# Operand addresses modulo 256 in a hybrid decoder trunk: a tile of its own for the first MLP's hidden parts, a pool of its own for the slots

## Chip, cores and metric

One core of one Trainium2 chip runs the whole program. The metric is the device time of one execution in microseconds (us). TensorE multiplies, VectorE (DVE) and ScalarE (ACT) prepare operands and take results out, GpSimd (POOL) and SyncE (SP) mostly issue DMAs. A matmul has two operands in SBUF: the weights, 128 columns that are loaded into the array (PEld in the profile), and the stream, 128 to 512 columns that run through it (PE).

## What is computed

512 tokens of width 1024 run through two layers: a latent attention (MLA) and a gated linear attention (GLA), each followed by a squared-ReLU MLP of width 4096, with RMS norms before each and at the end.

```python
for i in range(DEPTH):                        # DEPTH = 2
    xn = rms_norm(x, norm_mix[i])
    x = x + (mla_mixer(xn, ...) if i % 2 == 0 else gla_mixer(xn, ...))
    xn = rms_norm(x, norm_mlp[i])
    hid = jnp.square(jax.nn.relu(xn @ w_up[i]))
    x = x + hid @ w_down[i]
return rms_norm(x, final_norm)
```

## The kernel before

**Precision.** Operands are float32, and the matmuls run on a rounded form of it (float32r). Every operand is therefore split in a high part (ScalarE rounds it, L110) and a low part (VectorE subtracts, L113), and a product is three matmuls: wh·xh, wh·xl, wl·xh. `piece` splits a weight tile into `wh` and `wl`, each 1024 columns in a room of 1152, at the offset `at`; `signed` (L850, L851) splits with a sign or a gain; `slot("B")` gives one of 16 tiles of 512 columns.

**The MLPs.** Hidden columns come in eight blocks of 512. The first block's up product is plain (`up_first`, L118 to L120, 512 wide). All other up and down products go by a scheme of quadrants with seven products in place of eight (Strassen-Winograd): a block has seven up products (`up_product`, L973) and seven down products (`down_product`, L984 in the first MLP, L991 in the second). In the first MLP a product is 24 matmuls with a stream of 256; in the second MLP a down product is 12 matmuls with a stream of 512. The stream of a first MLP's down product is the hidden data, split by `parts_of_quad` into one of four pairs of slots (`parts_room`); the second MLP uses these pairs as weights. The eighth block's down product is plain again (L1242 in the first MLP, with a spare pair of parts in the buffer of the weight combination S1, tag `comb0`).

`step` treats block 0 with up and down products interleaved; `step_in_halves` treats blocks 1 to 6 with all up products first (168 matmuls in the first MLP), then all down products (168). In the down half the products are, in this order, d11, d22, d12, -d11, -dS1, d12, dS3; each of them needs the high and low parts of a hidden quadrant that VectorE combines shortly before (L1149 to L1163).

**Before block 0.** `quadrants` makes the input's combinations T1 to T4: L895 on ScalarE and L896 to L899 on VectorE for each of four pairs of feature tiles (the buffers are comb 2 to 5), then their split into the tile T (L850, L851). Weight combinations S1, dS1, dS3 and A2 are made by two DMAs each: SP brings one quadrant (L960), POOL adds the other on landing (L951, L962).

**Order.** The code is recorded instruction by instruction; a scheduler then sets each engine's order from the dependences. TensorE, ScalarE, VectorE, POOL and SP each take their own queue in order. A tile's place is fixed when it is allocated: pools are stacked, one behind the other, and a tile's byte address in a partition is the pool's place plus what stands before it, in steps of 32. A `gap` tile takes room and holds nothing.

**Addresses.** For each kind of matmul, the first byte of the stream and that of the weights, modulo 256, as the two programs place them:

| matmuls (line before, after) | number x width | before: stream / weights | after |
|---|---|---|---|
| up products, both MLPs (L973, L993) | 2352 x 256 | 208 / 16 | 208 / 16 |
| down products, first MLP (L984, L1006) | 1176 x 256 | 32 / 16 | 208 / 16 |
| down products, second MLP (L991, L1013) | 588 x 512 | 32 / 32 | 32 / 32 |
| first up products, both MLPs (L118 to L120, L132 to L134) | 192 x 512 | 208 / 208 | 208 / 16 |
| last down product, first MLP (L1242, L1264) | 72 x 512 and 24 x 512 | 32 / 32 and 224 / 32 | 208 / 16 |
| MLA, some of its products (L118 to L120, L680 to L684) | 368 of 128 to 512 | 32/128, 128/32, 192/32, 192/192 | 32 / 32 |
| MLA, GLA, output projections, the rest of L118 to L120 and L421 | about 1200, mostly 512 | 32 / 32 | 32 / 32 |
| GLA, own tiles (L1628, L1650) | 48 and 36 x 256 | 32 / 64 and 128 / 64 | 32 / 32 and 96 / 32 |
| GLA, states (L118 to L120) | 36 x 256 | 32 / 128 | 32 / 96 |

Of the kernel before, what the change touches and what calls it, by code (L numbers as in the profile page):

```python
# [10 lines left out]
F32 = mybir.dt.float32  # L11
# [7 lines left out]
P = 128  # L19
D = 1024  # L20
S = 512
# [29 lines left out]
def trunk_kernel(ctx: ExitStack, tc: tile.TileContext, t_in: dict, out: bass.AP):  # L51
# [39 lines left out]

    def slot(tag, shape=(P, 512)):
        return sb.tile(list(shape), F32R, tag=f"set_{tag}", bufs=16, name=uname("set"))


    X_AT = 44
    both_room = []

    def both_parts(i, at=0):
        if not both_room:  # L100
            both_room.append(sb.tile([P, 16 * S + 128], F32R, tag="set_A", bufs=1, name="set"))
        o = at + i * 2 * S
        return both_room[0][:, o : o + 2 * S].rearrange("p (a t) -> p a t", a=2)
# [39 lines left out]
    W_ROOM, W_AT = 1152, 128  # L143
    AT_X, AT_UP = (X_AT, X_AT), (124, 60)

# [241 lines left out]
    def mla(layer, nrm, first, pools):  # L387
# [3 lines left out]
        X = nrm.out  # L391
        (es, keep), (pre, pp) = pools


# [104 lines left out]
        for t in range(NT):  # L499
            tk = slice(t * P, (t + 1) * P)  # L500
            for hf in range(2):
                p = bank("bc"[hf])
                for k in range(2):
                    mm3(p, cut(CVL[k], slice(None), tk), cut(wv[k], slice(None), 0, slice(hf * 512, hf * 512 + 512)), k == 0, k == 1)
                if (t, hf) == (1, 1):
                    pr = bank("c")
                    for i in range(NT):
                        tr(pr[:, i * 3 * RB : (i + 1) * 3 * RB], rows[:, i * P : (i + 1) * P])
                    cols = keep.tile([P, NT, 3], F32, tag="cols", name="cols")
                    DVE.tensor_copy(cols, pr[:, : NT * 3 * RB].rearrange("p (t a r) -> p t a r", t=NT, a=3)[:, :, :, 0])  # L510
# [125 lines left out]
        HH = MH // 2  # L636
        QR = [f(slot("B", (P, 2, HH, 2, H))) for _ in range(NT)]
        QST = {}
# [176 lines left out]
    def mlp(layer, nrm, nxt=None):  # L815
# [7 lines left out]
        Q = [[[f(slot("B")) for _ in range(2)] for _ in range(2)] for _ in range(2)]  # L823
        parts_room = [(slot("B"), slot("B")) for _ in range(4)]
        turn = [0]
# [60 lines left out]
        def quadrants():  # L886
# [5 lines left out]
            for k in lead:  # L892
# [6 lines left out]
                DVE.scalar_tensor_tensor(t1[:, k], v[:, second], g2, t2[:, k], ALU.mult, ALU.subtract)  # L899
            fast.tile([P, 96], F32, tag="gap", name=uname("gap"))  # L900
            size = KH * 2 * TH
# [73 lines left out]
        def down_product(t, a, parts, start):  # L975
            wh, wl = piece(a, 2, 512, at=AT_UP if nxt else (W_AT, W_AT))
            if nxt:
                for j in range(4):
                    o = t[j // 2][:, j % 2 * TH : (j % 2 + 1) * TH] if isinstance(t, list) else t[:, j * TH : (j + 1) * TH]
                    for k in range(2):  # L980
                        xh, xl = cut(parts, slice(None), slice(k * TH, (k + 1) * TH))
                        a_h, a_l = (w_[:, k, j * P : (j + 1) * P] for w_ in (wh, wl))
                        for n, (w_, x_) in enumerate(((a_h, xh), (a_h, xl), (a_l, xh))):
                            PE.matmul(o, w_, x_, start=start and j % 2 == 0 and k == 0 and n == 0, stop=k == 1 and n == 2, skip_group_check=True)  # L984
                return
# [236 lines left out]
        if nxt:  # L1222
            spare = fast.tile([P, 2 * S], F32R, tag=f"comb{home['S1']}", bufs=1, name=uname("comb"))
            room = [parts_room[(turn[0] + k) % 4] for k in range(3)] + [(spare[:, :S], spare[:, S:])]
# [5 lines left out]
            for c in range(2):  # L1230
# [629 lines left out]
```

## Time and profile before

| | |
|---|---|
| median of 3 runs | 1052.44 us (1051.39 to 1053.14) |
| the profiled execution | 1051.57 us, its span 1049.9 us |
| granted TensorE clock | 0.999 |
| MLA and output projection | 0 to 184 us of the span |
| first MLP | 184 to 506 us (block 0 from 206.7, blocks 1 to 6 from 246.5 to 483.6) |
| GLA and output projection | 506 to 726 us |
| second MLP and final norm | 726 to 1050 us |

How to read it: times are from the start of the span. A row of the time line has the start, the time of the row, engine, line, operation, output<-inputs and the count. Matmuls overlap in the pipeline, so a matmul's own duration (276 ns at 256 columns) is longer than the distance to the next start. A row of windows has the stretch, its length, and for each engine the busy time and, in brackets, the instructions in it. A row of DMA issues ends with the median time from issue to landing.

### The profile page before, as it was taken

What the parts mean: (1) busy time and instruction counts of PE and PEld (TensorE: products, weight loads), DVE (VectorE), ACT (ScalarE), POOL (GpSimd) and SP (SyncE); (2) the same over time, 40 slices, a digit from 0 to 9 for tenths busy, and PEclk for the clock granted to TensorE, in tenths of its full rate; (3) what the DMA queues carried; (4) which work ended last, traced back from release to release, by engine and by line L of the source; (5) the groups of instructions that cost most, each with busy time, mean ns of one, the idle gap of its engine ahead of it and who ended that gap; (6) DMA issues with size and microseconds to landing.
All of it is one profiled execution on the core that took longest, in us unless ns stands there. A gap on an engine that the chain in (4) does not pass through costs nothing.

```text
span 1049.9 us, 16847 instructions
## 1 busy us (share of the span) xinstructions
PE 1039.6 (99%) x6522; PEld 930.1 (89%) x6522; DVE 881.2 (84%) x1343; ACT 697.7 (66%) x1122; POOL 113.9 (11%) x128
## 2 busy tenths in 40 slices
PE   9999999999999999999999999999999999999997
PEld 8788888899999999998888888888899889989985
DVE  7889977988988988989777389479798999898993
ACT  8667654667776776776445475665577777677784
POOL 8400010301101101100000000000011101111000
PEclk9999999999999999999999999999999999999999
DMA  7401234669688688632322221255488778778422
GB/s 232 121 21 41 81 100 141 161 173 224 173 196 198 164 200 197 149 97 81 91 80 82 81 81 41 81 140 160 102 222 205 179 209 192 192 199 189 120 81 81
DMA packets 120001, 145.85 MB, mean 139 GB/s; under 512 B 9488, under 2 KB 86288, under 8 KB 119920
## 3 DMA queue, kind: packets, MB, share of 16 engines
q1 hardware_dynamic: 95424, 113.57, 34.0%
q0 software_dynamic: 22400, 29.36, 17.7%
q10 hardware_dynamic: 2096, 1.84, 0.6%
q8 instruction: 51, 0.84, 0.3%
q14 instruction: 30, 0.25, 0.1%
HBM read 142.39 MB, written 2.10 MB: 138 GB/s over the span
## 4 chain that ended last, share of the span: by engine, by line
PE 91%; ACT 4%; DVE 4%; issue 1%; DMA 0%; ACTq 0%; SPq 0%; DVEq 0%
PE ps L973 24%; PE ps L984 12%; PE ps L991 11%; PE ps L118 10%; PE ps L120 10%; PE ps L119 10%; PE ps L1281 2%; PE ps L1242 2%; PE ps L1501 1%; PE ps L135 1%; PE ps L421 1%; DVE wl L113 1%; ACT wh L110 1%; PE ps L1628 1%; DVE set L113 1%
## 5 line engine op out<-in xcount | busy, mean ns | idle before, releaser
L110 ACT ACTIVATE wh<-wraw 128x1024 fp32r<-128x1024 f32 x139 | 146.9, 1060 | 133.0 <-issue 46.6
L113 DVE TENSOR_TENSOR wl<-wraw,wh 128x1024 fp32r<-128x1024 f32 x139 | 169.7, 1222 | 41.2 <-ACT wh L110 41.0
L973 PE MATMUL ps<-T,wh 128*128 128x256 f32 x896 | 154.8, 275 | 0.0
L110 ACT ACTIVATE wh<-comb 128x1024 fp32r<-128x1024 f32 x112 | 118.7, 1060 | 54.1 <-issue 28.7
L113 DVE TENSOR_TENSOR wl<-comb,wh 128x1024 fp32r<-128x1024 f32 x112 | 136.8, 1222 | 16.2 <-ACT wh L110 15.6
L984 PE MATMUL ps<-set,wh 128*128 128x256 f32 x784 | 142.5, 281 | 1.3 <-DVE set L851 1.1
L973 PEld LDWEIGHTS ps<-T,wh 128*128 128x128 f32 x896 | 135.2, 188 | 0.2
L973 PE MATMUL ps<-T,wl 128*128 128x256 f32 x448 | 123.3, 275 | 0.0
L984 PEld LDWEIGHTS ps<-set,wh 128*128 128x128 f32 x784 | 120.6, 188 | 2.8 <-DVE set L851 2.3
L991 PE MATMUL ps<-wh,set 128*128 128x512 f32 x392 | 122.9, 390 | 0.2 <-ACT set L110 0.2
L973 PE MATMUL ps<-set,wh 128*128 128x256 f32 x672 | 117.0, 276 | 0.0
L118 PE MATMUL ps<-set,wh 128*128 128x512 f32 x280 | 109.7, 392 | 0.0
L119 PE MATMUL ps<-set,wh 128*128 128x512 f32 x280 | 109.7, 392 | 0.0
L984 PE MATMUL ps<-set,wl 128*128 128x256 f32 x392 | 109.6, 280 | 0.0
L120 PE MATMUL ps<-set,wl 128*128 128x512 f32 x280 | 109.3, 390 | 0.0
L973 PEld LDWEIGHTS ps<-set,wh 128*128 128x128 f32 x672 | 102.0, 188 | 0.7
L973 PE MATMUL ps<-set,wl 128*128 128x256 f32 x336 | 92.7, 276 | 0.0
L991 PEld LDWEIGHTS ps<-wh,set 128*128 128x128 f32 x392 | 73.5, 188 | 15.4 <-ACT set L110 0.4
L973 PEld LDWEIGHTS ps<-T,wl 128*128 128x128 f32 x448 | 84.1, 188 | 0.0
L991 PE MATMUL ps<-wl,set 128*128 128x512 f32 x196 | 76.3, 389 | 0.0
L984 PEld LDWEIGHTS ps<-set,wl 128*128 128x128 f32 x392 | 73.5, 188 | 0.0
L973 PEld LDWEIGHTS ps<-set,wl 128*128 128x128 f32 x336 | 63.1, 188 | 0.0
(422 smaller groups left out, 2205.5 us busy)
## 6 DMA issues: line engine op xcount, KB each, us to landing
comb<-in_mlp_w_down_dram SPq DMA_DIRECT2D x74, 512.0 KB, 4.5
wraw<-in_mlp_w_up_dram SPq DMA_DIRECT2D x18, 1024.0 KB, 5.6
comb<-in_mlp_w_down_dram POOLq DMA_DIRECT2D x28, 512.0 KB, 7.1
wraw<-in_mlp_w_up_dram SPq DMA_DIRECT2D x28, 512.0 KB, 5.0
wraw<-in_gla_w_in_dram SPq DMA_DIRECT2D x12, 1024.0 KB, 5.2
comb<-in_mlp_w_up_dram SPq DMA_DIRECT2D x14, 512.0 KB, 4.1
comb<-in_mlp_w_up_dram POOLq DMA_DIRECT2D x14, 512.0 KB, 6.8
wraw<-in_mlp_w_up_dram POOLq DMA_DIRECT2D x14, 512.0 KB, 8.0
```

The costliest lines, as they stand in the source:

```text
L110: order(ACT.activation(hi, src, AF.Copy))
L113: lo_eng.tensor_tensor(lo, src, f(hi), ALU.subtract)
L118: PE.matmul(psum, wh, xh, start=start, stop=False)
L119: PE.matmul(psum, wh, xl, start=False, stop=False)
L120: PE.matmul(psum, wl, xh, start=False, stop=stop)
L135: PE.transpose(psum, src, ident[: src.shape[0], : src.shape[0]])
L421: PE.matmul(p, w[:, i, j * P : (j + 1) * P], x, start=start, stop=stop)
L973: PE.matmul(o, a_, x_, start=start and j == 0 and k == 0 and n == 0, stop=k == KH - 1 and n == 2, skip_group_check=True)
L984: PE.matmul(o, w_, x_, start=start and j % 2 == 0 and k == 0 and n == 0, stop=k == 1 and n == 2, skip_group_check=True)
L991: PE.matmul(o, x_, w_, start=start and k == 0 and n == 0, stop=k == 1 and n == 2, skip_group_check=True)
L1242: PE.matmul(p, a, x, start=k == 0 and n == 0, stop=k == 3 and n == 2)
L1281: PE.matmul(o, a, b_, start=False, stop=k == 3 and n == 2, skip_group_check=True)
```

## The change

The 16 slots get a pool of their own (`slot_layout`), with a gap in front; ahead of the first MLP it is closed and opened again at another address with 8 slots, and the hidden parts that the first MLP's down products stream lie in one tile behind them, 4 columns in. After that MLP the pool is laid out as before. Gaps in `keep` and in the MLPs' pool, and `cols` in another pool, move the other tiles. The first up products' weights and the last down products' weights go to the offsets `AT_UP`; the last product's spare parts lie in T's tile. `down_product` of the first MLP runs its loops in another order: for each half of the output, all wh·xh, then all wl·xh, then all wh·xl.

```diff
-    def slot(tag, shape=(P, 512)):
-        return sb.tile(list(shape), F32R, tag=f"set_{tag}", bufs=16, name=uname("set"))
+    SLOT_AT, SLOT_AT_FAR, KEEP_AT = 56, 32, 32
+    slots = {}
+
+    def slot_layout(at, bufs=16):
+        if slots:
+            slots["es"].close()
+        es = slots["es"] = ExitStack()
+        slots["bufs"] = bufs
+        slots["pool"] = es.enter_context(tc.tile_pool(name=uname("slots"), bufs=1, reuse_waits="tile"))
+        if at:
+            slots["pool"].tile([P, at], F32, tag="gap", name=uname("gap"))
+
+    ctx.callback(lambda: slots["es"].close())
+    slot_layout(SLOT_AT)
+
+    def slot(tag):
+        return slots["pool"].tile([P, S], F32R, tag=f"set_{tag}", bufs=slots["bufs"], name=uname("set"))
...
-            both_room.append(sb.tile([P, 16 * S + 128], F32R, tag="set_A", bufs=1, name="set"))
+            both_room.append(sb.tile([P, 16 * S + 64], F32R, tag="set_A", bufs=1, name="set"))
...
+        keep.tile([P, KEEP_AT], F32, tag="gap", name="gap_keep")
...
-                    cols = keep.tile([P, NT, 3], F32, tag="cols", name="cols")
+                    cols = rk.tile([P, NT, 3], F32, name="cols")
...
-        parts_room = [(slot("B"), slot("B")) for _ in range(4)]
+        if nxt:
+            parts_tile = slots["pool"].tile([P, 8 * S + 8], F32R, tag="parts", name="hidden_parts")
+            halves_ = [parts_tile[:, 4 + i * S : 4 + (i + 1) * S] for i in range(8)]
+            parts_room = [(halves_[2 * i], halves_[2 * i + 1]) for i in range(4)]
+        else:
+            parts_room = [(slot("B"), slot("B")) for _ in range(4)]
...
-                w = [piece(raw[:, :, j * P : (j + 1) * P], ND, P, at=AT_X) for j in range(2)]
+                w = [piece(raw[:, :, j * P : (j + 1) * P], ND, P, at=AT_UP) for j in range(2)]
...
-            fast.tile([P, 96], F32, tag="gap", name=uname("gap"))
+            fast.tile([P, 120 if nxt else 104], F32, tag="gap", name=uname("gap"))
...
             if nxt:
-                for j in range(4):
-                    o = ...
-                    for k in range(2):
-                        xh, xl = cut(parts, slice(None), slice(k * TH, (k + 1) * TH))
-                        a_h, a_l = (w_[:, k, j * P : (j + 1) * P] for w_ in (wh, wl))
-                        for n, (w_, x_) in enumerate(((a_h, xh), (a_h, xl), (a_l, xh))):
-                            PE.matmul(o, w_, x_, ...)
+                xh, xl = parts
+                for i in range(2):
+                    for n, (w_, x_) in enumerate(((wh, xh), (wl, xh), (wh, xl))):
+                        for j in (2 * i, 2 * i + 1):
+                            o = ...
+                            for k in range(2):
+                                ts = slice(k * TH, (k + 1) * TH)
+                                PE.matmul(o, w_[:, k, j * P : (j + 1) * P], x_[:, ts], ...)
...
-            spare = fast.tile([P, 2 * S], F32R, tag=f"comb{home['S1']}", bufs=1, name=uname("comb"))
+            spare = fast.tile([P, 8 * KH * TH + 4], F32R, tag="T", name=uname("T"))[:, 4 : 4 + 2 * S]
...
-                        w = piece(last_raw[c][:, :, j * P : (j + 2) * P], 4, 256)
+                        w = piece(last_raw[c][:, :, j * P : (j + 2) * P], 4, 256, at=AT_UP)
...
     psum_layout("quad")
+    slot_layout(SLOT_AT_FAR, 8)
     mlp(0, n_mlp0, n_mix1)
     psum_layout(False)
+    slot_layout(SLOT_AT)
```

What it moves in the engines' orders, at four places. First TensorE, the first MLP's first down product, from the end of the up product ahead of it; before (set_2146 is the high part of the hidden data, set_2147 the low part; the last three rows go on in the same way to 24):

```order
L973 MATMUL ps_2361<-set,wh_2362 128x256 x2
L973 MATMUL ps_2361<-set,wl_2363 128x256
L984 MATMUL ps_515_2392<-set_2146,wh_2395 128x256
L984 MATMUL ps_515_2392<-set_2147,wh_2395 128x256
L984 MATMUL ps_515_2392<-set_2146,wl_2396 128x256
```

and after (the 8 in the third row are the low part's four of the first output half and the high part's four of the second):

```order
L993 MATMUL ps_2364<-set,wl_2366 128x256
L1006 MATMUL ps_511_2395<-hidden_parts,wh_2398 128x256 x4
L1006 MATMUL ps_511_2395<-hidden_parts,wl_2399 128x256 x4
L1006 MATMUL ps_511_2395<-hidden_parts,wh_2398 128x256 x8
L1006 MATMUL ps_511_2395<-hidden_parts,wl_2399 128x256 x4
```

The low part, read by the second matmul before, is read from the ninth on; the low weights move from the third matmul to the fifth.

Second VectorE in block 1's down half, ahead of the fifth product, whose low part is written by L851 (before) or L871 (after) from `set_2145` or `set_2155`; before:

```order
L1150 TENSOR_TENSOR set_2139<-set_2141,set_2139 128x512
L113 TENSOR_TENSOR wl_3219<-comb_2796,wh_3218 128x1024
L113 TENSOR_TENSOR set_2153<-set_2145,set_2152 128x512
L1163 TENSOR_TENSOR set_2145<-set_2145,set_2142 128x512
L113 TENSOR_TENSOR wl_3252<-comb_2622,wh_3251 128x1024
L113 TENSOR_TENSOR set_2149<-set_2143,set_2148 128x512
L1157 TENSOR_TENSOR xT<-ps_596_3099,xT 128x4x256
L113 TENSOR_TENSOR wl_3285<-comb_2725,wh_3284 128x1024
L851 SCALAR_TENSOR_TENSOR set_2147<-set_2145,set_2146 128x512
```

and after:

```order
L1172 TENSOR_TENSOR set_2149<-set_2151,set_2149 128x512
L127 TENSOR_TENSOR hidden_parts<-set_2155,hidden_parts 128x512
L1185 TENSOR_TENSOR set_2155<-set_2155,set_2152 128x512
L127 TENSOR_TENSOR wl_3222<-comb_2799,wh_3221 128x1024
L127 TENSOR_TENSOR hidden_parts<-set_2153,hidden_parts 128x512
L127 TENSOR_TENSOR wl_3255<-comb_2625,wh_3254 128x1024
L1179 TENSOR_TENSOR xT<-ps_592_3102,xT 128x4x256
L871 SCALAR_TENSOR_TENSOR hidden_parts<-set_2155,hidden_parts 128x512
L127 TENSOR_TENSOR wl_3288<-comb_2728,wh_3287 128x1024
```

The low part of the fifth product stands one weight split (of the seventh product's weights) earlier.

Third VectorE at the end of the MLA's output projection, where it adds a product to x (L800, after L815) and splits the first MLP's input and weights; before:

```order
L800 TENSOR_TENSOR xT<-ps_1969,xT 128x512
L896 SCALAR_TENSOR_TENSOR comb_2306<-xT,gains,comb_2306 128x256
L113 TENSOR_TENSOR wl_2158<-wraw_2155,wh_2157 128x1024
L263 SCALAR_TENSOR_TENSOR set<-xT,gains,set 128x512
L252 TENSOR_TENSOR acc_1883<-acc_1883,tmp_2026 128x512
L897 SCALAR_TENSOR_TENSOR comb_2305<-xT,gains,comb_2306 128x256
L898 SCALAR_TENSOR_TENSOR comb_2307<-xT,gains,comb_2305 128x256
L899 SCALAR_TENSOR_TENSOR comb_2304<-xT,gains,comb_2305 128x256
```

and after, at the last of four such additions:

```order
L815 TENSOR_TENSOR xT<-ps_2051,xT 128x512
L127 TENSOR_TENSOR wl_2246<-wraw_2239,wh_2245 128x1024
L277 SCALAR_TENSOR_TENSOR set<-xT,gains,set 128x512
L266 TENSOR_TENSOR acc_1888<-acc_1888,tmp_2109 128x512
L916 SCALAR_TENSOR_TENSOR comb_2309<-xT,gains,comb_2309 128x256 x2
L917 SCALAR_TENSOR_TENSOR comb_2308<-xT,gains,comb_2309 128x256
L127 TENSOR_TENSOR tmp_2113<-acc_1888,tmp_2112 128x512
L918 SCALAR_TENSOR_TENSOR comb_2310<-xT,gains,comb_2308 128x256
```

All 16 quadrant rows (two in the row that is counted twice) stand behind the last sum of squares; before, 13 of them stood ahead of it.

Fourth SP's queue at the same place; before:

```order
L140 DMA wraw_2035<-in_mla_w_o_dram 128x8x256
L960 DMA comb_2340<-in_mlp_w_up_dram 128x4x256
L960 DMA comb_2343<-in_mlp_w_down_dram 128x2x512
L140 DMA wraw_2155<-in_mlp_w_up_dram 128x8x256
L140 DMA wraw_2236<-in_mlp_w_up_dram 128x8x256
L140 DMA wraw_2348<-in_mlp_w_up_dram 128x8x256
```

and after:

```order
L154 DMA wraw_2040<-in_mla_w_o_dram 128x8x256
L154 DMA wraw_2158<-in_mlp_w_up_dram 128x8x256
L154 DMA wraw_2239<-in_mlp_w_up_dram 128x8x256
L154 DMA wraw_2351<-in_mlp_w_up_dram 128x8x256
L980 DMA comb_2343<-in_mlp_w_up_dram 128x4x256
L980 DMA comb_2346<-in_mlp_w_down_dram 128x2x512
```

The first loads of S1 and dS1 go behind three loads of up weights. On POOL dS1's second load goes behind the 12 instructions that make the GLA's masks.

More of the change, by code (lines that the diff above doesn't have):

```diff
@@ L143, in trunk_kernel @@
     W_ROOM, W_AT = 1152, 128
-    AT_X, AT_UP = (X_AT, X_AT), (124, 60)
+    AT_UP = (124, 60)
     def room_for(tag, a, n, at=W_AT):
@@ L636, in mla @@
         HH = MH // 2
-        QR = [f(slot("B", (P, 2, HH, 2, H))) for _ in range(NT)]
+        QR = [f(slot("B")).rearrange("p (g h a c) -> p g h a c", g=2, h=HH, a=2) for _ in range(NT)]
         QST = {}
@@ L977, in down_product @@
             if nxt:
-                for j in range(4):
-                    o = t[j // 2][:, j % 2 * TH : (j % 2 + 1) * TH] if isinstance(t, list) else t[:, j * TH : (j + 1) * TH]
-                    for k in range(2):
-                        xh, xl = cut(parts, slice(None), slice(k * TH, (k + 1) * TH))
-                        a_h, a_l = (w_[:, k, j * P : (j + 1) * P] for w_ in (wh, wl))
-                        for n, (w_, x_) in enumerate(((a_h, xh), (a_h, xl), (a_l, xh))):
-                            PE.matmul(o, w_, x_, start=start and j % 2 == 0 and k == 0 and n == 0, stop=k == 1 and n == 2, skip_group_check=True)
+                xh, xl = parts
+                for i in range(2):
+                    for n, (w_, x_) in enumerate(((wh, xh), (wl, xh), (wh, xl))):
+                        for j in (2 * i, 2 * i + 1):
+                            o = t[i][:, j % 2 * TH : (j % 2 + 1) * TH] if isinstance(t, list) else t[:, j * TH : (j + 1) * TH]
+                            for k in range(2):
+                                ts = slice(k * TH, (k + 1) * TH)
+                                opens = start and j % 2 == 0 and k == 0 and n == 0
+                                PE.matmul(o, w_[:, k, j * P : (j + 1) * P], x_[:, ts], start=opens, stop=k == 1 and n == 2, skip_group_check=True)
                 return
```

## The prediction

> **What bounds the kernel now.** I read the page first, then the time line of TensorE, since the page already says where the time is.
>
> ```profile
> span 1049.9 us, 16847 instructions
> PE 1039.6 (99%) x6522; PEld 930.1 (89%) x6522; DVE 881.2 (84%) x1343; ACT 697.7 (66%) x1122; POOL 113.9 (11%) x128
> PE 91%; ACT 4%; DVE 4%; issue 1%; DMA 0%; ACTq 0%; SPq 0%; DVEq 0%
> L984 PE MATMUL ps<-set,wh 128*128 128x256 f32 x784 | 142.5, 281 | 1.3 <-DVE set L851 1.1
> ```
>
> TensorE is busy 99% and carries 91% of the chain, so what counts is the pace of its matmuls. L984, the first MLP's down products, also waits for VectorE (last column, us). Its mean of 281 ns holds pipeline time that overlaps; the cost of a matmul is the distance to the next start. So next are first starts of runs, in the first MLP's blocks 1, 2 and 6, then in the second MLP.
>
> ```profile
> 265.60 0.28 PE L984 MATMUL ps<-set,wh 128*128 128x256 f32 x1
> ...
> 277.11 0.40 PE L984 MATMUL ps<-set,wh 128*128 128x256 f32 x2
> 277.67 0.39 PE L984 MATMUL ps<-set,wh 128*128 128x256 f32 x1 [0.17 <-DVE set L851]
> 277.90 0.28 PE L984 MATMUL ps<-set,wl 128*128 128x256 f32 x1
> ...
> 286.00 0.28 PE L973 MATMUL ps<-set,wh 128*128 128x256 f32 x1
> ...
> 305.08 0.40 PE L984 MATMUL ps<-set,wh 128*128 128x256 f32 x2
> ...
> 463.09 0.28 PE L984 MATMUL ps<-set,wh 128*128 128x256 f32 x1
> ...
> 483.60 0.40 PE L1242 MATMUL ps<-set,wh 128*128 128x512 f32 x1
> ...
> 810.81 0.40 PE L991 MATMUL ps<-wh,set 128*128 128x512 f32 x1
> ...
> 829.89 0.28 PE L973 MATMUL ps<-set,wh 128*128 128x256 f32 x1
> ```
>
> A block's 168 up matmuls take 286.00 to 305.08, 19.08 us, 113.6 ns each (streamed/weights at 208/16). Its 168 down matmuls take 265.60 to 286.00, 20.40 us (20.51 in block 6). The second MLP's 84 wide down matmuls, the same number of columns, take 19.08 again, 227.1 each (32/32). So 0.443 ns a column is the pace that this program reaches, and the first MLP's down half is 1.32 us off it per block. Part is a wait: the pair at 277.11 should be followed 0.23 later, is followed after 0.56, and the next start comes 0.23 instead of 0.12 on: 0.44 in all, for the low part that L851 writes on VectorE. The rest, 0.88 over 168, is 5.2 ns on every matmul.
>
> That the 5.2 ns go with addresses is seen on one line. L118 to L120 at 32/32 (16.86 to 33.18, 72 matmuls), at 32/128 (V products, 51.12 to 59.31, 35) and at 208/208 (184.09 to 191.08, 30, then 191.54 to 206.73, 66):
>
> ```profile
> 16.86 0.39 PE L118 MATMUL ps<-set,wh 128*128 128x512 f32 x1
> 33.18 0.39 PE L459 MATMUL ps<-set,wh 128*128 128x512 f32 x1
> 51.12 0.39 PE L119 MATMUL ps<-wl,cq0h 128*128 128x512 f32 x1
> 59.31 0.39 PE L118 MATMUL ps<-cq0h,wh 128*128 128x512 f32 x1
> 184.09 0.40 PE L118 MATMUL ps<-set,wh 128*128 128x512 f32 x1
> 191.08 0.63 PE L277 MATMUL ps<-tmp,inv 128*128 128x512 f32 x2
> 191.54 0.39 PE L118 MATMUL ps<-set,wh 128*128 128x512 f32 x1
> 206.73 0.40 PE L973 MATMUL ps<-set,wh 128*128 128x256 f32 x2
> 594.02 0.40 PE L1628 MATMUL ps<-set,ADh 128*128 128x256 f32 x2
> 595.44 0.28 PE L118 MATMUL ps<-set,kth 128*128 128x256 f32 x1
> ```
>
> They take 226.7, 234.0, 233.0 and 230.2 ns; L1628, 256 wide at 32/64, takes 1.42 us for 12, 118.3. A bad pair costs 5 to 7 ns whatever the width, which looks like a fixed collision between the weight load and the stream.
>
> The Trainium skill, "TensorE: Matmul & The Clock Gate", section "Step-by-step: what each phase is for", speaks against this: TensorE has two independent SBUF read ports, and "Loading the next tile's weights doesn't steal SBUF read bandwidth from the running matmul." By it the addresses would be worth nothing and only waits would go (first rival, 1049.4). The rows above disagree with it, so I go by the rows.
>
> **The change, part by part.**
>
> *Down products of the first MLP, blocks 1 to 6.* Streams go from 32/16 to 208/16, the up products' own pair, 113.6 ns. The low part xl is wanted at the ninth matmul, 8 x 0.1136 = 0.91 us after a product starts, instead of 0.23; it came 0.33 late, so 0.68 more covers it, and VectorE's new order writes it one weight split earlier. What is now wanted earlier is nothing but order: wl goes from third to fifth. Six blocks: the first is 20.40, the last 20.51, together 122.7; 6 x 19.08 = 114.5. Gain 8.2, of it 2.6 waits. It needs VectorE to keep up at 38.2 us a block; the second MLP does:
>
> ```profile
> 868.00:906.20 38.20, 38.20 (x253) 34.87 (x253) 35.09 (x39) 28.29 (x40) 5.50 (x5) 1.00 0.77 194
> 283.40:322.90 39.50, 39.34 (x339) 39.13 (x338) 35.29 (x39) 28.37 (x40) 4.95 (x4) 1.00 0.78 187
> ```
>
> The columns after the stretch are TensorE, its weight loads, VectorE, ScalarE, POOL: VectorE has 35.1 us of work there and 35.3 here.
>
> *Block 0 of the first MLP*, 206.73 (above) to 246.53 (below): 39.80 us for 336 matmuls; at 113.6 they take 38.17. Gain 1.6. It includes a wait before an L984 at 217.49.
>
> ```profile
> 217.00 0.28 PE L973 MATMUL ps<-T,wl 128*128 128x256 f32 x1
> 217.49 0.39 PE L984 MATMUL ps<-set,wh 128*128 128x256 f32 x1 [0.21 <-ACT set L110]
> ...
> 246.53 0.28 PE L973 MATMUL ps<-set,wh 128*128 128x256 f32 x1
> ```
>
> *Entry of the first MLP.* Thirteen of VectorE's 16 quadrant rows (L896 to L899, 0.40 to 0.51 us from start to start) leave their places among the output projection's rows and stand behind its last sum:
>
> ```profile
> 168.69 0.48 DVE L896 SCALAR_TENSOR_TENSOR comb<-xT,gains,comb 128x256 f32<-128x256 f32 x1
> ...
> 183.29 0.48 DVE L899 SCALAR_TENSOR_TENSOR comb<-xT,gains,comb 128x256 f32<-128x256 f32 x1
> ...
> 187.30 0.76 DVE L252 TENSOR_TENSOR acc<-acc,tmp 128x512 f32<-128x512 f32 x1
> ...
> 196.97 1.22 DVE L113 TENSOR_TENSOR wl<-wraw,wh 128x1024 fp32r<-128x1024 f32 x1
> ```
>
> Today the low weights of block 0's first up product start at 196.97, 9.8 us before their product at 206.73. In the new order, from about 187.5: 16 quadrant rows 6.8, one split 0.7, four T parts 4.6, three of the rsqrt 1.9, three hidden rows 1.8, one residual row 1.1, then these weights 1.1: ready at 205.5. The product would start at 206.3 and want them at 206.5. Covered by 1.0 us: cost nothing, but thin; if the cover is gone, it is paid one for one.
> SP's queue moves too; these are its issues of today and the times to landing:
>
> ```profile
> 147.74 0.37 SPq L960 DMA_DIRECT2D comb<-in_mlp_w_up_dram  x1
> ...
> 155.32 20.82 SPq L140 DMA_DIRECT2D wraw<-in_mlp_w_up_dram  x3
> ...
> comb<-in_mlp_w_up_dram SPq DMA_DIRECT2D x14, 512.0 KB, 4.1
> comb<-in_mlp_w_up_dram POOLq DMA_DIRECT2D x14, 512.0 KB, 6.8
> ```
>
> S1 and dS1 now go out behind the three loads, after 176.1 instead of at 147.74. S1's second half waits on POOL for the first to land, about 181 to 183, with the GLA masks and dS1's second half queued behind it, and lands about 190; VectorE adds S1 at about 209. Cost nothing, covered by 19 us. The last products' spare parts take T's place instead of the S1 buffer's; T's last reader in block 6 ends at 463.1, 20 us before they are read: nothing.
>
> *First up products, both MLPs*, 208/208 to 208/16, 512 wide. No row has that pair at that width. From 226.7 (both 256-wide at 208/16 and wide at 32/32 run at 0.443 a column) to 233.0: 96 x 2 at 226.7 gain 0.84, at 233.0 lose 0.4. I take 0.8, by the pair that is nearest.
>
> *Last products, L1242*, 483.60 to 505.70: 22.10 us, 96 x 226.7 = 21.8. Gain 0.3, with the same doubt.
>
> ```profile
> 505.70 0.39 PE L118 MATMUL ps<-set,wh 128*128 128x512 f32 x1
> ```
>
> *MLA*: 368 matmuls leave bad pairs for 32/32, at 5 to 7 ns: 2.2 us if TensorE alone sets the pace, 0 if every one hides in a wait. TensorE is busy 146.22 of the first 148 us, so I take two thirds, 1.4.
>
> ```profile
> 0.00:148.00 148.00, 146.22 (x743) 121.50 (x744) 128.63 (x326) 101.77 (x219) 35.26 (x58) 1.00 0.32 95
> ```
>
> *GLA*: 48 of L1628's 84 go to 32/32, 48 x 5 = 0.2. The other 36, and 36 that go to 32/96, have no row: between a loss of 0.2 and a gain of 0.4, taken as 0. Gap tiles and pool borders issue nothing.
>
> Sum: 8.2 + 1.6 + 0.8 + 0.3 + 1.4 + 0.2 = 12.5. The profiled execution took 1051.57 (span 1049.9); the median of the runs is 0.87 above that, 1052.44. So 1039.1 against the profile, 1039.9 as a median, said as 1040.0.
>
> **Rivals.**
>
> 1. *The 5 ns are not the addresses'* but lie in how the down products mix operands; the change then doesn't do what it says. Only waits go: 6 x 0.44, and 0.4 in block 0: 3.0, time 1049.4. For it: L984 differs from L973 in more than addresses. Against it: one and the same line, L118, at two paces.
> 2. *VectorE's backlog at the entry reaches TensorE.* 13 rows, 5.5 us, over a cover of 1.0. For it: VectorE has hardly a gap from 184 to 208. Against it: my count ends before the need. It costs up to 4.5 to 5.5: 1040 to 1045.
> 3. *The new loop order is itself slow*, and the end is slower. Each pair of matmuls now changes to the other half of the PSUM bank. The waits bring 3.0 and the other places 2.7, so a result 2.1 us slower needs 1176 matmuls dearer by (3.0 + 2.7 + 2.1)/1176 = 6.6 ns than today's 118.8, that is 125.4 ns. At 126 ns: 8.5 - 5.7 = 2.8 more, 1055.2. Against it: L421 changes its bank with every matmul and takes 3.17 us for 14 from 13.69 to 16.86, 226.4.
>
> ```profile
> 13.69 1.07 PE L421 MATMUL ps<-set,wh 128*128 128x512 f32 x4
> ```
>
> 4. *A part of the pace*: 208/16 suits only the up products' rhythm, and down products land near 116: 2.8 less, 1042.7.
>
> **How the numbers follow.** Forecast 0.70 (1038 to 1042); rival 2, 0.13; rival 4, 0.08; rival 1, 0.06; rival 3, 0.03. The low end takes MLA's 2.2, GLA's 0.4 and the spread of the runs, about 0.9: 1037.8; the high end is rival 2's, 1045. That leaves out rivals 1 and 3 and a little of the rest, under 0.2. 0.2% is 2.1 us, about what a measurement of this kernel tells from no change. Forecast, rivals 2 and 4 and most of rival 1 are faster by more: 0.93; the rest of rival 1 and of 3 is the same, 0.04; slower 0.03.
>
> **What would show it.** Right: the six down runs of the first MLP take 19.1 us each with no wait for L871 (the old L851); block 0 takes 38.2; the first up products 226.7 a matmul. Wrong: L1006 still at 118 (rival 1) or above (rival 3), or a gap on TensorE between 206 and 225 put down to VectorE's weight splits (rival 2).

## The result and the profile after

| kernel, on one chip | median us (range) | ratio to before, 95% interval |
|---|---|---|
| before | 1052.76 (1051.39 to 1053.14) | |
| changed | 1042.48 (1041.71 to 1043.77) | 0.9906 (0.9889 to 0.9923) |

The change gains 10.3 us, where 12.4 were forecast (1040.0 against 1052.44). The first lines of the page of the changed kernel (span, engines, chain, one group of down products):

```profile
span 1040.8 us, 16839 instructions
PE 1030.6 (99%) x6522; PEld 923.2 (89%) x6522; DVE 878.5 (84%) x1343; ACT 695.1 (67%) x1122; POOL 113.2 (11%) x128
PE 92%; DVE 4%; ACT 2%; DMA 1%; issue 1%; SPq 0%; ACTq 0%; DVEq 0%
L1006 PE MATMUL ps<-hidden_parts,wh 128*128 128x256 f32 x784 | 106.6, 275 | 0.0
```

TensorE's 6522 matmuls are the same, and their busy time fell by 9.0 us. The down products no longer wait for VectorE: the last column of L1006, once L984, is 0.0, and the mean of one fell from 281 to 275 ns. First starts of runs in blocks 1, 2 and 6 (the numbers changed: L973 is L993, L984 is L1006, L1242 is L1264, L118 to L120 are L132 to L134):

```profile
264.78 0.28 PE L1006 MATMUL ps<-hidden_parts,wh 128*128 128x256 f32 x1
...
283.82 0.28 PE L993 MATMUL ps<-set,wh 128*128 128x256 f32 x1
...
302.86 0.28 PE L1006 MATMUL ps<-hidden_parts,wh 128*128 128x256 f32 x1
...
455.18 0.39 PE L1006 MATMUL ps<-hidden_parts,wh 128*128 128x256 f32 x2
...
474.22 0.39 PE L1264 MATMUL ps<-hidden_parts,wh 128*128 128x512 f32 x1
```

264.78 to 283.82 and 455.18 to 474.22 are both 19.04 us for 168 matmuls, 113.3 ns each, as long as the up half between 283.82 and 302.86. All six down runs took that.

Both kernels issue the same number of matmuls in the same places, so the n-th start in one trace can be set against the n-th in the other. Worked out so (TensorE's starts, us; a minus is a gain):

| stretch | forecast | changed, first profile | changed, second profile (e7) | e1_entry |
|---|---|---|---|---|
| first weights arrive | 0 | +0.39 | +0.23 | +0.22 |
| MLA | -1.4 | -0.46 | -0.47 | -0.60 |
| first up products, both MLPs | -0.8 | -0.67 | -0.67 | -0.67 |
| block 0 of the first MLP | -1.6 | -0.41 | -0.21 | -1.70 |
| blocks 1 to 6 | -8.2 | -8.59 | -8.59 | -8.59 |
| last products of the first MLP | -0.3 | -0.02 | -0.01 | +0.08 |
| output projections, GLA | -0.2 | -0.09 | -0.16 | -0.24 |
| second MLP, up to its last sums | 0 | +0.78 | +0.04 | +0.72 |
| sum, with 0 or -0.05 in the tail | -12.5 | -9.05 | -9.89 | -10.78 |

The forecast's sum falls short in three places: block 0 (1.2), the MLA (0.9) and 1.2 in waits for loads.

Block 0, in the time line of TensorE, shows the first of these. It ran from 206.35 to 245.74, 39.40 us, not 38.17:

```profile
206.35 0.40 PE L993 MATMUL ps<-set,wh 128*128 128x256 f32 x2
...
212.04 0.30 PEld L993 LDWEIGHTS ps<-set,wh 128*128 128x128 f32 x2 [0.26 <-ACT ps L1041]
...
228.87 0.50 PE L993 MATMUL ps<-set,wh 128*128 128x256 f32 x2 [0.24 <-ACT ps L1075]
...
245.74 0.28 PE L993 MATMUL ps<-set,wh 128*128 128x256 f32 x1
```

Up products wait for ScalarE, which copies the PSUM bank that they go on with (L1041, L1075). What ScalarE was doing, and what it waited for:

```profile
201.73 1.07 ACT L124 ACTIVATE wh<-comb 128x1024 fp32r<-128x1024 f32 x1 [2.40 <-DMA comb<-in_mlp_w_down_dram]
...
209.73 0.73 ACT L902 ACTIVATE set<-tmp 128x256 f32<-128x256 f32 x2 [2.34 <-DVE tmp L900]
210.36 1.14 ACT L124 ACTIVATE hidden_parts<-set 128x512 fp32r<-128x512 f32 x2
211.40 0.58 ACT L1041 ACTIVATE ps<-ps 128x512 f32<-128x512 f32 x1
...
227.03 1.30 ACT L870 ACTIVATE hidden_parts<-set 128x512 fp32r<-128x512 f32 x2 [1.78 <-DVE set L1088]
228.23 0.58 ACT L1075 ACTIVATE ps<-ps 128x512 f32<-128x512 f32 x1
```

Each copy stands in ScalarE's queue behind a row that waits for VectorE: 2.34 us for L900 and 1.78 for L1088. (The first row, a wait for a load, comes back under e1.) And VectorE is behind from the entry on:

```profile
187.77 0.87 DVE L916 SCALAR_TENSOR_TENSOR comb<-xT,gains,comb 128x256 f32<-128x256 f32 x2
...
194.60 0.48 DVE L919 SCALAR_TENSOR_TENSOR comb<-xT,gains,comb 128x256 f32<-128x256 f32 x1
...
204.27 1.21 DVE L127 TENSOR_TENSOR wl<-wraw,wh 128x1024 fp32r<-128x1024 f32 x1
206.13 0.69 DVE L127 TENSOR_TENSOR hidden_parts<-set,hidden_parts 128x512 fp32r<-128x512 f32 x1 [0.65 <-ACT hidden_parts L124]
...
209.01 0.68 DVE L900 SCALAR_TENSOR_TENSOR tmp<-ps,rstd 128x512 f32<-128x512 f32 x1
```

The 16 quadrant rows fill 187.77 to 195; the low weights of block 0's first product are ready at 205.5, as forecast; the last row of L900 starts at 209.01, before the change (as L880) at 206.93. The 0.65 us ahead of 206.13 are VectorE's only wait from 187 to 236.

The wait in the second MLP is one for the last but one load of down weights:

```profile
1005.06 0.63 ACT L124 ACTIVATE set<-comb 128x512 fp32r<-128x512 f32 x1 [0.84 <-DMA comb<-in_mlp_w_down_dram]
...
1012.01 1.67 PE L1303 MATMUL ps<-set,set 128*128 128x512 f32 x6 [0.99 <-ACT ps L1272]
```

SP issued it at 1000.75, and at 1010.59 in the kernel before, in the same place of the same queue; this time it landed later.

### The profile page after: what moved, and what is told of

Its sections match the earlier page's. It is cut to its first block, busy times and chain, and to the rows that moved or that the text cites. A ratio compares the mean times of both kernels' runs of the same rounds, so it can differ in the third digit from the quotient of the medians.

```text
span 1040.8 us, 16839 instructions
## 1 busy us (share of the span) xinstructions
PE 1030.6 (99%) x6522; PEld 923.2 (89%) x6522; DVE 878.5 (84%) x1343; ACT 695.1 (67%) x1122; POOL 113.2 (11%) x128
## 4 chain that ended last, share of the span: by engine, by line
PE 92%; DVE 4%; ACT 2%; DMA 1%; issue 1%; SPq 0%; ACTq 0%; DVEq 0%
PE ps L993 25%; PE ps L1006 12%; PE ps L1013 12%; PE ps L132 10%; PE ps L133 10%; PE ps L134 10%; PE ps L1303 2%; PE ps L1264 2%; PE ps L149 1%; PE ps L1523 1%; PE ps L436 1%; PE ps L1650 1%; DVE wl L127 1%; ACT wh L124 1%; DMA comb<-in_mlp_w_down_dram 1%
## 5 line engine op out<-in xcount | busy, mean ns | idle before, releaser
L993 PE MATMUL ps<-T,wh 128*128 128x256 f32 x896 | 154.8, 275 | 0.1
L993 PEld LDWEIGHTS ps<-T,wh 128*128 128x128 f32 x896 | 135.1, 188 | 0.5 <-ACT tmp L1101 0.3
L993 PE MATMUL ps<-T,wl 128*128 128x256 f32 x448 | 123.3, 275 | 0.0
L993 PE MATMUL ps<-set,wh 128*128 128x256 f32 x672 | 117.0, 276 | 0.3 <-ACT ps L1075 0.2
L132 PE MATMUL ps<-set,wh 128*128 128x512 f32 x280 | 109.6, 391 | 0.0
L134 PE MATMUL ps<-set,wl 128*128 128x512 f32 x280 | 109.2, 390 | 0.0
L1006 PE MATMUL ps<-hidden_parts,wh 128*128 128x256 f32 x784 | 106.6, 275 | 0.0
L993 PEld LDWEIGHTS ps<-set,wh 128*128 128x128 f32 x672 | 101.9, 188 | 1.4 <-ACT ps L1075 0.4
L1006 PEld LDWEIGHTS ps<-hidden_parts,wh 128*128 128x128 f32 x784 | 97.0, 188 | 0.0
L993 PE MATMUL ps<-set,wl 128*128 128x256 f32 x336 | 92.6, 276 | 0.0
L993 PEld LDWEIGHTS ps<-T,wl 128*128 128x128 f32 x448 | 84.1, 188 | 0.0
L993 PEld LDWEIGHTS ps<-set,wl 128*128 128x128 f32 x336 | 63.1, 188 | 0.0
L134 PEld LDWEIGHTS ps<-set,wl 128*128 128x128 f32 x280 | 52.6, 188 | 11.0
L133 PEld LDWEIGHTS ps<-set,wh 128*128 128x128 f32 x280 | 52.6, 188 | 10.9 <-DVE set L765 0.2
```

Of the source, the lines that this page charges most:

```text
L132: PE.matmul(psum, wh, xh, start=start, stop=False)
L133: PE.matmul(psum, wh, xl, start=False, stop=False)
L134: PE.matmul(psum, wl, xh, start=False, stop=stop)
L993: PE.matmul(o, a_, x_, start=start and j == 0 and k == 0 and n == 0, stop=k == KH - 1 and n == 2, skip_group_check=True)
L1006: PE.matmul(o, w_[:, k, j * P : (j + 1) * P], x_[:, ts], start=opens, stop=k == 1 and n == 2, skip_group_check=True)
```

## Experiments

All on the chip, each beside runs of the kernel before, which took 1051.79 us (median) beside e1 to e4, 1051.60 beside e5 to e8 and 1052.39 beside e9. Medians of different series are therefore compared by their gains over it. Stretches are worked out from first starts as above.

**e1_entry: the order at the entry alone.** The changed kernel's pool of slots ends at byte 164576, the old one ended at 164640. So `sum5`, the first tile of the MLP's pool, covers the last 64 bytes of the sixteenth old slot. With the pool made longer by 96 bytes and the gap in front of T shorter by as much, the quadrant rows and the loads of S1 and dS1 go back to their old places, and no matmul changes its address or place.

```diff
-            parts_tile = slots["pool"].tile([P, 8 * S + 8], ...)
+            parts_tile = slots["pool"].tile([P, 8 * S + 32], ...)
-            fast.tile([P, 120 if nxt else 104], ...)
+            fast.tile([P, 96 if nxt else 104], ...)
```

> The changed kernel with 24 more columns behind the hidden parts and 24 fewer in the MLP's gap, so that sum5 no longer covers the last 64 bytes of the sixteenth old slot. Every matmul keeps its addresses and TensorE its order; the quadrant rows go back among the output projection's rows, and S1 and dS1 to the front of SP's queue. My theory: block 0's lost microsecond is VectorE's backlog of 13 rows, 5.5 us. Then L993 no longer waits for ScalarE at 212, 229 and 237, block 0 falls from 39.40 to 38.2 to 38.5, and the median is 0.9 to 1.2 us under the changed kernel's. Rival: those waits belong to the new loop order of the down products or to the first loads of w_down; block 0 stays at 39.4 and the time at that of the changed kernel.

Measured: 1040.56 us (1040.08 to 1040.81), ratio 0.9891 (0.9876 to 0.9907). Block 0:

```profile
205.98 0.40 PE L993 MATMUL ps<-set,wh 128*128 128x256 f32 x2
...
244.07 0.39 PE L993 MATMUL ps<-set,wh 128*128 128x256 f32 x2
```

38.09 us, 336 matmuls at 113.4. The busy time from 206 to 250 in the changed kernel (the columns after the length are TensorE, weight loads, VectorE, ScalarE, POOL):

```profile
206.00:250.00 44.00, 43.60 (x377) 42.93 (x376) 42.99 (x49) 31.05 (x42) 5.69 (x5) 1.00 0.73 181
```

and in e1_entry:

```profile
206.00:250.00 44.00, 44.00 (x390) 44.00 (x389) 40.21 (x47) 32.63 (x43) 5.03 (x4) 1.00 0.77 191
```

VectorE is idle for 1.0 us of the 44 in the changed kernel and for 3.8 here, where TensorE has no gap left. The block's missing 1.3 us come from the order at the entry, and that from 64 bytes. Since the loads of S1 and dS1 and the masks moved back together with the rows, the run alone doesn't tell what share these loads had. The trace of the changed kernel speaks against a large one: neither ScalarE nor VectorE waits for S1 or dS1 there. The load for which ScalarE waited up to 201.73 is another one of down weights. SP issued it at 196.24 (it took 5.4 us), the same load of the kernel before at 189.68, and what SP had waited for was VectorE's L871 behind the quadrant rows. First the issue before the change, then the one after it, and SP's wait (total, times, longest, us):

```profile
189.68 0.37 SPq L960 DMA_DIRECT2D comb<-in_mlp_w_down_dram  x1
196.24 0.37 SPq L980 DMA_DIRECT2D comb<-in_mlp_w_down_dram  x1
SPq L980 <- DVE T L871: 8.7, 1, 8.7
```

So by the trace this wait too goes back to the rows; a run that moves the rows without the loads wasn't made.

**e2_parts_at_32: the address alone.** e1_entry with the streams of the down products back at 32 modulo 256:

```diff
-            halves_ = [parts_tile[:, 4 + i * S : 4 + (i + 1) * S] for i in range(8)]
+            halves_ = [parts_tile[:, 24 + i * S : 24 + (i + 1) * S] for i in range(8)]
```

> The kernel of e1_entry with one number changed: the hidden parts begin 24 columns into their tile in place of 4, so the first MLP's down products stream from 32 in place of 208 modulo 256, weights at 16 as before; all five engines' orders are the same. Theory (the pair of addresses sets the pace): the down runs of blocks 1 to 6 go from 19.04 to 19.9 us, 118.3 to 118.8 ns a matmul; 1176 x 5.2 ns = 6.1 us slower than e1_entry, within 0.5. Rival (the loop order sets the pace): 19.04 as in e1_entry, no difference in time.

Measured: 1048.21 us (1047.55 to 1048.98), 7.65 more than e1_entry for one number, where 6.1 were expected (e3 shows what was left out). Block 1's down half:

```profile
264.46 0.40 PE L1006 MATMUL ps<-hidden_parts,wh 128*128 128x256 f32 x2
...
284.61 0.28 PE L993 MATMUL ps<-set,wh 128*128 128x256 f32 x1
```

20.15 us, 120.0 ns a matmul, 6.6 more than at 208/16. The Trainium skill, "SBUF — State Buffer", section "SBUF: two separate sides", states that "PE, ACT, and DVE's dedicated pair never wait on anyone". This run doesn't test that: what costs 6.6 ns on each of 1176 matmuls is the start address of TensorE's own stream, and m1_map below shows such costs with no other engine at work.

**e3_order_only: the loop order alone.** The kernel before with the new loops in `down_product` (the piece of the diff above that begins with `if nxt:` and takes out the old loops).

> The kernel before with the new loop order of the first MLP's down products alone; addresses stay 32/16. Theory: the waits for the low part go, the pace stays; down runs of 19.9 to 20.0 us (168 x 118.6) in place of 20.44, six blocks and block 0 together 3.0 us faster than before. Rival one (the order sets the pace): 19.05 a run, about 8.4 us faster. Rival two (alternating halves of a PSUM bank are slow): over 20.44 a run, slower than before.

Measured: 1050.22 us (1049.44 to 1050.73), ratio 0.9984 (0.9975 to 0.9992): 1.6 us, half of what was expected. The runs have no wait left, yet take 20.15 us, 120.0 ns:

```profile
266.10 0.28 PE L986 MATMUL ps<-set,wh 128*128 128x256 f32 x1
...
286.25 0.28 PE L973 MATMUL ps<-set,wh 128*128 128x256 f32 x1
```

The old order ran at (20.40 - 0.44)/168 = 118.8 at these addresses, so at 32/16 the new order costs 1.2 ns a matmul, 0.2 of the 0.44 us a block that it saves. At 208/16 it costs nothing (19.04). So rival 3's effect exists at 32/16, and is 1.2 ns in place of the 6.6 that it needed. It also explains why e2 lost more than was expected.

**e4_old_order: the addresses with the old loop order.** e1_entry with the old loops.

> The kernel of e1_entry with the old loop order of the down products; addresses stay 208/16. Theory: between the waits the pace stays 113.3 ns, and the low part is again wanted by the second matmul, so each down run waits 0.4 to 0.6 us: 19.5 to 19.7 us in place of 19.04, 2.6 to 4 us slower than e1_entry in all. Rival (the order sets the pace): 20.4 a run, 8 us slower than e1_entry. If VectorE keeps ahead without the new order: 19.04, the same time as e1_entry.

Measured: 1045.91 us (1045.02 to 1046.04), 5.35 more than e1_entry, where 2.6 to 4 were expected. Block 1's down half is 20.00 us with one wait:

```profile
263.10 0.28 PE L1004 MATMUL ps<-hidden_parts,wh 128*128 128x256 f32 x1
...
275.03 0.38 PE L1004 MATMUL ps<-hidden_parts,wh 128*128 128x256 f32 x1 [0.66 <-DVE hidden_parts L871]
...
283.10 0.28 PE L993 MATMUL ps<-set,wh 128*128 128x256 f32 x1
```

The pace outside the wait is that of e1_entry (113.5); the wait is 20.00 - 19.04 = 0.96 us, twice the old 0.44. TensorE now comes to the fifth product 10.88 us after the run's start in place of 11.51, 0.6 sooner, and VectorE, with 18.6 us of work in these 20, ends L871 only 0.1 sooner (11.9 in place of 12.0). With before (1051.79 in this series), e3 and e1 this makes a square: the order alone brings 1.6, the addresses (with the entry in its old order) 5.9, both 11.2. The order is worth 1.6 at the old addresses and 5.4 at the new ones.

**m1_map: the pairs by themselves.** Not the trunk, but 6656 matmuls back to back, for 16 stream and 16 weight starts:

```python
for n, count in ((256, 12), (512, 8)):
    for si in range(16):
        for wi in range(16):
            for m in range(count):
                xo = 64 + 4 * si + m % 2 * 512
                wo = 64 + 4 * wi + m % 4 * 128
                PE.matmul(bank[:, :n], weights[:, wo : wo + P], room[:, xo : xo + n], ...)
```

> Not the trunk: nothing of it is computed and zeros are written out. Only matmuls, back to back, no waits: 12 of 256 columns, then 8 of 512, for each of 16 stream starts and 16 weight starts modulo 256 in steps of 16 bytes; streams alternate between two places 2048 bytes apart, weights run through four places 512 bytes apart; then 256 columns again with weights at 144 and 160 and 64 stream starts over 1024 bytes. Theory: the distance from start to start is 113.3 ns at 208/16 and 118 to 120 at 32/16, and 32/32 is slow at 256 columns (119 in the GLA's rows) and fast at 512 (227), so there is no rule by the pair alone, the width counts too; and the last part repeats every 256 bytes. Rival: bad pairs cost their 5 to 7 ns only amid the trunk's other traffic, and here every pair takes 113.3 and 226.7. Second rival: the period is not 256, and the last part shows another one.

Measured, in one run: ns from start to start, from a set's second start to its last, the median of the eight pairs of a difference (stream less weights, modulo 256). The first two rows are for streams that start at a multiple of 32, the others for streams 16 off:

```
difference     0    16    32    48    64    80    96   112   128   144   160   176   192   208   224   240
256, x 32  119.5 119.9 116.7 116.8 117.8 118.1 120.1 119.7 118.2 119.8 119.0 118.8 113.7 117.7 118.2 118.2
512, x 32  226.7 228.1 233.3 233.2 233.3 230.8 233.0 233.7 233.3 232.7 234.5 231.7 233.3 233.3 233.0 226.7
256, +16   118.1 116.7 118.6 118.7 118.2 120.1 119.0 118.2 120.0 116.6 116.5 119.4 115.7 118.9 119.8 116.9
512, +16   231.2 230.8 232.3 233.3 226.7 231.1 233.3 231.2 232.7 233.3 232.5 233.3 228.8 230.0 226.7 236.7
```

In the first row the pairs of one difference agree within 0.5 ns in 12 of 16 columns (the program's first two sets, which began at 213 ns, left out). So what counts is the difference, together with whether the stream starts at a multiple of 32, and it needs no other engine's traffic. At 256 columns 192 is the only good difference in this table. At 512 columns 0 and 240 are good for streams at multiples of 32, 64 and 224 for those 16 off. So in these short sets no pair suits both widths. The streams over 1024 bytes repeated every 256, within 0.8 ns. One more thing is seen in single distances: 208/16 began with 121, 118, 118, 118, 118, 119 and then ran at 113; 32/16 changed between 117 and 123 throughout. A good pair settles after some matmuls (in e4, behind the wait in block 1, six take 118 to 119 before 113 comes back). And 224/160 ran at 117.7 in the first part and at 113.3 throughout in the last, as 16/160 (a difference of 112) did there: what came before counts too.

**e5_weights_at_96: another pair of difference 192.** e3_order_only with other offsets for the down products' weights:

```diff
-            wh, wl = piece(a, 2, 512, at=AT_UP if nxt else (W_AT, W_AT))
+            wh, wl = piece(a, 2, 512, at=(80, 80) if nxt else (W_AT, W_AT))
```

> The kernel of e3_order_only with two numbers changed: the weights of the first MLP's down products begin 80 columns into their rooms in place of 124 and 60, so they lie at 96 modulo 256 in place of 16; the hidden parts stay at 32, in the slots, where they were before. All five engines' orders are the same. Theory (what counts at 256 columns is stream less weights, and 192 is the good difference: 208 - 16, and 32 - 96 modulo 256): down runs of 19.0 to 19.1 us in place of 20.15, 1176 x 6.6 = 7.8 us faster than e3_order_only, about 1042.5. Rival (the stream has to leave 32, where the other operands lie): 20.0 to 20.2 a run as in e3_order_only, 1050.

Measured: 1042.55 us (1042.47 to 1044.05), ratio 0.9914 (0.9901 to 0.9928). That is 9.05 less than before, where e3_order_only brought 1.57: 7.5 for the offsets, and level with the whole change beside it (e7, 0.9917). Block 1's down half, streams where they always were:

```profile
264.98 0.28 PE L986 MATMUL ps<-set,wh 128*128 128x256 f32 x1
...
284.03 0.28 PE L973 MATMUL ps<-set,wh 128*128 128x256 f32 x1
```

19.05 us. A pool of slots, gaps and a tile of its own weren't needed for these 7.5 us; two offsets of the weights give them.

**e9_parts_at_80: a difference of 64 in a long run.** e1_entry with 36 in place of 4 columns (8 more in the tile, 8 fewer in the gap).

> The kernel of e1_entry with the hidden parts 36 columns into their tile in place of 4: streams of the first MLP's down products at 80, weights at 16, a difference of 64; orders the same, gaps moved by 8 columns. In the map of pairs this difference took 117.7 ns on the mean, but one row of the map's last part (stream 224, weights 160, also 64) ran at 113.3 throughout, while the same pair ran at 117.7 in the map's first part. Theory one (192 is the only difference that a long run of 256-column matmuls settles into): down runs of 19.7 to 19.9 us, 5 to 6 us slower than e1_entry. Theory two (a long run settles into 113.3 at 64 as well, and what came before decides): 19.04 to 19.1, the time of e1_entry.

Measured: 1047.05 us (1046.62 to 1047.47), 5.3 less than before, where e1_entry brought 11.2: 5.9 slower, as theory one has it. Block 1's down half:

```profile
264.56 0.28 PE L1006 MATMUL ps<-hidden_parts,wh 128*128 128x256 f32 x1
...
284.45 0.28 PE L993 MATMUL ps<-set,wh 128*128 128x256 f32 x1
```

All six down runs take 19.89 us, 118.4 ns, and none settled. In the trunk 192 is what a run of 168 needs, of the three differences tried (16, 64, 192).

**e6_wide_at_240: 512 columns at 208/240.** e1_entry with the wide products' weights moved:

```diff
-                w = [piece(raw[:, :, j * P : (j + 1) * P], ND, P, at=AT_UP) for j in range(2)]
+                w = [piece(raw[:, :, j * P : (j + 1) * P], ND, P, at=(52, 52)) for j in range(2)]
...
-                        w = piece(last_raw[c][:, :, j * P : (j + 2) * P], 4, 256, at=AT_UP)
+                        w = piece(last_raw[c][:, :, j * P : (j + 2) * P], 4, 256, at=(52, 52))
```

> The kernel of e1_entry with the weights of the first up products of both MLPs and of the first MLP's last down product at 240 in place of 16 modulo 256, streams at 208 as they are; orders the same. Theory (the map's 512-column table has 226.7 at 208/240 and 228.8 at 208/16): 226.7 a matmul in place of 227.5 (192) and 230 (96), 0.4 to 0.5 us less, 1040.1. Rival (the map doesn't carry over to the trunk's sequence of operands): no change, or 0.3 us more.

Measured: 1040.75 us (1039.64 to 1041.46), the same as e8_entry_again beside it. The first up products go from 227.5 to 227.3 ns, the last ones from 230.1 to 229.7: 0.1 us in all, a miss for the time. But the map does carry over. The first 71 distances of the last products take 226.8 at 208/240 (nearly all 226 or 227) and 228.9 at 208/16 (225, 231, 231), as in the map. The 0.15 us of these are given back at one place, the 73rd product; here the first and the 73rd, in e6 and then in e8:

```profile
471.94 0.62 PE L1264 MATMUL ps<-hidden_parts,wh 128*128 128x512 f32 x2
...
488.45 0.70 PE L1264 MATMUL ps<-hidden_parts,wh 128*128 128x512 f32 x2
...
471.77 0.62 PE L1264 MATMUL ps<-hidden_parts,wh 128*128 128x512 f32 x2
...
488.28 0.69 PE L1264 MATMUL ps<-hidden_parts,wh 128*128 128x512 f32 x2
```

It starts 16.51 us after the first in both, 0.14 behind the end of an addition on VectorE (L1266), for which it most likely waits. In the first up products the first 30 go from 229.0 to 227.0 too, the next 20 starts lose as much, and the last 48 took 226.7 at 208/16 already, in place of the map's 228.8. So in the trunk 208/16 reached the good pace at both widths, and why it did so there and not in the first 30 wasn't tried.

**e7_changed_again and e8_entry_again: what comes and goes.** The changed kernel and e1_entry, unaltered, side by side.

> The changed kernel itself, unaltered, beside the next one on one chip. Theory: block 0 again 39.4 with the three waits of L993 for ScalarE, 1.3 us more than e8_entry_again in that stretch; the wait for the last w_down piece before the last sums of squares (0.8 us in the first trace) comes and goes between executions, like the first loads, and is no part of the change. Rival: that wait is there again and belongs to the change; then it is also in e8_entry_again.

> The kernel of e1_entry unaltered, beside e7_changed_again on one chip. Theory: its median is 1.0 to 1.5 us under that of e7_changed_again, block 0 is 38.1 again. Rival: the two medians differ by less than 0.5 us, since the gain in block 0 is given back behind it.

Measured: 1042.77 us (1041.67 to 1044.38), ratio 0.9917 (0.9903 to 0.9930), and 1040.73 (1039.81 to 1040.94), 0.9895 (0.9881 to 0.9908). Block 0 is 39.59 and 38.10. The medians lie 2.0 apart, more than the 1.5 of block 0; the rest isn't explained, the ranges are as wide. The wait for the late load of down weights is gone in e7 (+0.04 in the table), was there in e1 (+0.72) and again in the same code of e8 (+0.56), and is +0.06 and +0.25 in e2 and e4, whose code is the same there: it belongs to executions. (Another late load, of up weights, cost 1.5 us in e5's profile alone.) So do the first loads, -0.48 to +0.94 over all profiles. e1_entry is the fastest version found.

## Why the prediction was right, and where not

The time, 1042.48, lies in the stated range, but above the part of it that the forecast's own mechanism was given (1038 to 1042): the sum was 2.1 us too large, in the main by items 2 and 3.

1. *Blocks 1 to 6 (8.2)*: measured 8.59, of it 8.4 in the down runs (122.66 before, 6 x 19.04 after); the up runs gave the rest. Shown by e2 and e5: the pace goes with the difference of the two addresses, so rival 1 is out. That a bad pair costs the same "whatever the width" is wrong by the map, and that the cause is a collision between the weight load and the stream is not shown: the runs show the dependence on the addresses, not what happens inside TensorE. That the total came out so close is partly luck. The split into 2.6 for waits and 5.6 for the pace was wrong, since the two aren't independent: the order alone brought 1.75 in these blocks (e3), the addresses without it 3.25 (e4).
2. *Block 0 (1.6)*: measured 0.41. The step that failed is the entry's "cost nothing". Its count was right as far as it went: the low weights were ready at 205.5. It stopped at the first product, and looked only for TensorE waiting on a weight split. But VectorE is idle for no more than 0.65 us before 236 and can't catch up, so the 13 rows were still late behind the first product, and reached TensorE through ScalarE's queue. Rival 2 came true at 1.3 us in place of 4.5 to 5.5. That the order at the entry costs it is shown by e1; that it is the rows and not the moved loads is read from the trace.
3. *MLA (1.4)*: measured 0.46. The step that failed is "368 matmuls leave bad pairs for 32/32, at 5 to 7 ns": 32/32 had been read from rows of 512 columns alone. The 36 V products, 512 wide, got their gain:

```profile
51.56 0.39 PE L133 MATMUL ps<-wl,cq0h 128*128 128x512 f32 x1
...
59.52 0.39 PE L132 MATMUL ps<-cq0h,wh 128*128 128x512 f32 x1
```

   35 in 7.96 us, 227.4 in place of 234.0. The other 512-wide ones went only from 245 to 243 on the mean, waits included, and the 144 of 128 to 384 columns gained nothing (0.1 us more in all). The map agrees: a difference of 0 takes 119.5 at 256 columns. Beyond the V products' 0.23 us little is clear of noise: e3 and e5, whose MLA is that of the kernel before, stand at -0.29 and +0.05 in this stretch.
4. *GLA (0.2)*: the 48 products that went to 32/32 at 256 columns take 119.3 in place of 118.1, for the same reason; 0.1 in all came from elsewhere.
5. *First up products (0.8)*: 0.67, from 231.0 to 227.5 ns (229.1 in the first 30 of each MLP, 226.8 in the other 66); the pair that had no row lay near the good end. *Last products (0.3)*: 0.02, since 208/16 took 228.9 there, between the two ends, and 230.1 with the wait at the 73rd.
6. The forecast left out that an execution can lose or win about a microsecond at its loads. The medians differ by 10.3 and the two profiles by 9.05, because the profile before (1051.57) lay 1.2 under the median of the runs beside the changed kernel (1052.76) and the profile after (1042.52) on its own.

## What to carry over

Where matmuls follow each other without waits, compare the distances of the same width at different start addresses before looking for a rule, and count the difference of stream and weights modulo 256. For this data type the good ones were 192 at 256 columns, and at 512 columns 0 or 240 for streams at multiples of 32, 64 or 224 for streams 16 off. One number in one offset can be the whole gain, but measure it in the kernel: a wait behind it can take the gain back (e6). After a change of pools compare the order of every engine, since an overlap of 64 bytes moved 13 rows and cost over a microsecond. When work is moved onto a busy engine, follow its lateness to the first gap in which that engine can catch up, and through the queues of those that wait for it, not to the first reader alone.

## What the runs showed that was not expected

- The pace of a matmul depends on the difference of the two start addresses modulo 256, on the width, and on whether the stream starts at a multiple of 32. For streams that do, the map has 113.7 ns at 192 and 116.7 to 120.1 elsewhere at 256 columns, 226.7 at 0 and 240 and 228.1 to 234.5 elsewhere at 512.
- A good pair needs some matmuls to settle (121, 118, 118, 118, 118, 119, then 113 at 208/16), and a bad one can alternate (117, 123 at 32/16). The same pair can run at two paces: 208/16 at 512 columns took 229.1 in 30 products and 226.7 in 48 others of the same kernel.
- At 32/16 the order of operands matters by 1.2 ns (118.8 against 120.0), at 208/16 hardly (113.5 outside the wait against 113.3).
